# Feed-forward by seven products: the chain to one operand goes first, and twelve low parts go to GpSimd

## The chip, the cores and the metric

One core of a Trainium2 chip runs the whole program. The metric is the device time of one execution in microseconds (us); runs of one kernel are compared by their medians. The engines of the core work side by side, each through its own queue in order: TensorE (PE in the profile; its weight loads are PEld), VectorE (DVE), ScalarE (ACT), GpSimd (POOL) and SyncE (SP), which here only issues DMAs.

## The reference

One layer of a streaming encoder over 576 tokens (512 of a prompt and 64 of a sample): a combined projection, two kinds of attention, an output projection with a layer norm, a feed-forward block with a layer norm, and a gated embedding. All in float32. The part that the change touches is the feed-forward block:

```
x   = LN1(alpha * x + mix @ w_o)
hid = square(relu(x @ w_up))          # 1024 -> 4096
x   = LN2(alpha * x + hid @ w_down)   # 4096 -> 1024
```

## The kernel before

**Numbers.** TensorE multiplies float32 values as pairs: a high part (the value rounded by a copy to the matmul's type, made by ScalarE) and a low part (value minus high part, made by VectorE with one `tensor_tensor`). A product takes three matmuls per block of 128: weight high with operand high, weight high with operand low, weight low with operand high, in this order. Weights are split in the same way: a DMA brings a raw piece (`wraw`), ScalarE copies it to the high half of `whl` (line 149), VectorE makes the low half (line 155).

**Feed-forward groups.** The 4096 hidden values are worked in eight groups `g` of 512. Groups 0 and 1 go up by plain products. From then on the 2x2 block scheme with seven products in place of eight is used: an even and an odd group make a pair of row blocks, the token halves A and B (288 each) the columns. The stage runs over a list of "pairs" of output blocks, each with seven products of 12 matmuls: first four down-pairs of group 1, then for g = 2 and 4 two up-pairs of g, two up-pairs of g+1 and four down-pairs of g+1, then the four up-pairs of groups 6 and 7. Groups 6 and 7 go down by plain products.

The seven products of a pair come in the order `11, t0, t1, 21, t3, t2, 22`. On the operand's side they read these sums, each with a high and a low part:

```
ROWS = {"11": "11", "t3": "s1", "t0": "s3", "21": "12", "t1": "s2", "22": "s4", "t2": "22"}
```

For the down-pairs these sums are made of the hidden values by `operands` (line 1341): `11` and `s3` when the even group is done, and `s2`, `s1`, `22`, `12` and `s4` when the odd group's values come out, for each half `m` = 0, 1 of the group's columns (an up-pair each in groups 3 and 5). They lie in tiles `hA` (`s3`, `11`), `hB` (`12`, `22`), `hC` (`s1`, `s2`), `hD` (`s4`) and `hF` (the plain hidden values of the even group and running sums). The half m = 0 of an operand is read by the first six matmuls of a product, m = 1 by the last six.

The values of the second token half of an odd group come out of the product t2: line 1558 adds the last partial sum from PSUM (`r<-n,r`), line 1560 does relu and square in one VectorE instruction, line 1372 makes the sum s2 (`hF<-hF,r`), line 1351 copies its high part (ScalarE), line 1349 makes the low part (VectorE). Line 1374 makes s1, line 1379 makes s4 from `12` and the sum before, in place of `12`. In the down-pairs, lines 1585, 1587, 1596 and 1599 add products from PSUM to the layer's output `Y`.

**Order.** Two things set the order on each engine. The program emits these steps through a list (`later(delay, fn)`, up to three a clock, a clock being six matmuls), between them steps of the weights (`WT.step`), which also issue the loads: SP brings a raw piece, and GpSimd's queue issues a DMA that adds a second piece to it in place (line 210, one a pair). Then the framework's scheduler orders every engine's instructions at build time: of those that it reckons to be ready, the one written first goes first; inside `tc.high_priority()` they go ahead of the others. The matmuls of the seven products are pinned to the program's order. On the chip each engine takes its list in order and waits on semaphores.

Of the kernel before, what the change touches and what calls it, by code (L numbers as in the profile page):

```python
# [11 lines left out]
OP = mybir.AluOpType  # L12
# [24 lines left out]
def tile_hybrid_step(ctx: ExitStack, tc: tile.TileContext, I, O):  # L37
    nc = tc.nc
    PE, ACT, DVE, POOL, SP = nc.tensor, nc.scalar, nc.vector, nc.gpsimd, nc.sync
# [4 lines left out]
    def f(ap):  # L44
        return ap.bitcast(F32)
# [16 lines left out]
    def later(delay, fn):  # L62
        number[0] += 1
        evq.append((clock[0] + delay, number[0], fn))
# [52 lines left out]
    class Weights:  # L117
# [23 lines left out]
        def split(self, u, src, cuts, eng):  # L141
            lo_at = [0]

            def high(c):
                def fn():
                    if c is cuts[0]:
                        self.slot(u)
                        lo_at[0] = clock[0] + 2
                    ACT.copy(self.hv[u][:, 0, c], src["tile"][:, c])  # L149
                return fn  # L150

            def low(c):
                def fn():
                    t = self.hv[u]
                    eng.tensor_tensor(t[:, 1, c], src["tile"][:, c], f(t[:, 0, c]), OP.subtract)  # L155
                    if c is cuts[-1]:
                        self.done.add(u)
                return fn
            for c in cuts:
                self.piece(u, None, high(c), src)  # L160
            for c in cuts:
                self.piece(u, lo_at if len(cuts) == 1 else None, low(c), src)
# [1149 lines left out]
    HX, late = {}, []  # L1312

    def sets(g):

        if g >= G_DOWN:
            hid[g] = base.tile([128, 2, 4, NT], F32R, name="hidE", tag="AL") if g % 2 == 0 else \
                fb.tile([128, 2, 4, NT], F32R, name="hidO", tag="hidO")
            return
        names = ("s3", "11") if g % 2 == 0 else ("12", "22")  # L1320
        t = base.tile([128, 2, 2, 4, HW], F32R, name="hA", tag="AL") if g % 2 == 0 else \
            fb.tile([128, 2, 2, 4, HW], F32R, name="hB", tag="hidO")
        for i, n in enumerate(names):
            HX[n] = [t[:, i, x] for x in range(2)]
        if g % 2 == 0:
            HX["f"] = fs.tile([128, 2, 4, HW], F32, name="hF")
# [13 lines left out]
    def operands(g, m, t, v):  # L1340

        b = slice(2 * m, 2 * m + 2)
        tt = DVE.tensor_tensor

        def split(n, v, d=0):
            owed[n] = owed.get(n, 0) + 1

            def low():
                tt(HX[n][1][:, b], v, f(HX[n][0][:, b]), OP.subtract)
                owed[n] -= 1  # L1350
            later(d, lambda: ACT.copy(HX[n][0][:, b], v))
            later(d, low)

        if g >= G_DOWN:
            oh, ol = [hid[g][:, x, b, (A, B)[t]] for x in range(2)]
            later(0, lambda: ACT.copy(oh, v))
            later(0, lambda: DVE.tensor_tensor(ol, v, f(oh), OP.subtract))
            return
        F = [HX["f"][:, x, b] for x in range(2)]
        if g % 2 == 0:  # L1360
            if t == 0:
                split("11", v)
            if t == (g == 0):
                later(3, lambda: tt(F[0], F[0], F[1], OP.subtract))
                split("s3", F[0], 3)
            return
        if t == 1:
            if m == 0:
                later(0, more_sets)
                if g > 1:  # L1370
                    later(0, last_set)
            later(0, lambda: DVE.scalar_tensor_tensor(F[0], F[0], -1.0, v, op0=OP.mult, op1=OP.subtract))
            split("s2", F[0])
            later(1, lambda: tt(F[1], F[1], v, OP.subtract))
            split("s1", F[1], 1)
            split("22", v, 3)
            return
        split("12", v)
        later(2, lambda: tt(v, v, F[0], OP.add))
        if g > 1:  # L1380
            split("s4", v, 2)
        else:
            late.append(lambda: split("s4", v, 2))

    def up_half(g, c, m, sl):
        t = (A, B).index(sl)
        r = lnp[0].tile([128, 2, 320], F32, name="relu", bufs=2)[:, :, :HW]
        out = HX["f"][:, t, c:c + 2]
        later(0, lambda: ACT.activation(r, m[:, :, :HW], AF.Relu))
        later(0, lambda: ACT.activation(out, r, AF.Square))  # L1390
        operands(g, c // 2, t, out)

    def up_evac(g, c, m):
        if c == 0:
            HX["r"] = fs.tile([128, 2, 2, HW], F32, name="r", bufs=2)
        rr = HX["r"]
        r = rr[:, :, c]
        later(0, lambda: ACT.activation(r, m[:, :, :HW], AF.Relu))
        later(0, lambda: ACT.activation(r, r, AF.Square))
        if c:  # L1400
            for t in (1, 0):
                operands(g, 0, t, rr[:, t])

    def up(g, lns=None):
# [28 lines left out]
        for t in (1, 0):  # L1433
            m = psum_g()
            for c in range(2):
                for _ in gemm(m[:, c, :HW], Ws[c], range(8), BH, BL, (A, B)[t]):
                    WT.step()
                    yield 1
            later(0, lambda t=t, m=m: ACT.activation(rr[:, t], m[:, :, :HW], AF.Relu))
            later(0, lambda t=t: ACT.activation(rr[:, t], rr[:, t], AF.Square))  # L1440
            operands(g, 1, t, rr[:, t])
# [84 lines left out]
    def owe(P, fn):  # L1526
        def do():
            fn()
            P.left -= 1
        P.left += 1  # L1530
        later(0, do)

    def settle(P):
        while P.left:
            pop_now()

    def up_pair(g, m):

        P = Pair(U["P", g // 2, g % 2 * 2 + m], SX)
        b = slice(2 * m, 2 * m + 2)  # L1540
        tt = DVE.tensor_tensor
        if m == 0:
            P.start = lambda: sets(g)

        def target(t):
            return HX["f"][:, t, b] if g < G_DOWN and g % 2 == 0 else P.r[:, t]

        def t0():
            P.r = fs.tile([128, 2, 2, HW], F32, name="r", bufs=2)
            owe(P, lambda: ACT.copy(P.r[:, 1, 0], P.z))  # L1550

        def t3():
            settle(P)
            with tc.high_priority():
                tt(P.r[:, 1, 1], P.e, P.r[:, 1, 0], OP.subtract)

        def t2():
            tt(P.r[:, 1, 0], P.o, P.r[:, 1, 0], OP.add)
            if g % 2:
                later(0, lambda: DVE.scalar_tensor_tensor(target(1), P.r[:, 1], 0.0, P.r[:, 1], op0=OP.max, op1=OP.mult))  # L1560
            else:
                later(0, lambda: ACT.activation(P.r[:, 1], P.r[:, 1], AF.Relu))
                later(0, lambda: ACT.activation(target(1), P.r[:, 1], AF.Square))
            operands(g, m, 1, target(1))

        def s21():
            later(0, lambda: ACT.activation(P.r[:, 0, 0], P.d, AF.Relu))

        def s22():
            later(0, lambda: ACT.activation(P.r[:, 0, 1], P.e, AF.Relu))  # L1570
            later(0, lambda: ACT.activation(target(0), P.r[:, 0], AF.Square))
            operands(g, m, 0, target(0))
        P.posts = {"t0": t0, "21": s21, "t3": t3, "t2": t2, "22": s22}
        return P

# [257 lines left out]
```

## Time and profile before

| what | value |
|---|---|
| median of 3 runs | 765.87 us (765.47 to 766.1) |
| the profiled execution | 765.81 us, its span 764.1 us |
| TensorE busy | 751.4 us (98%) |
| VectorE busy | 571.4 us (75%) |
| ScalarE busy | 472.6 us (62%) |
| GpSimd busy | 110.6 us (14%) |

Busy time is the time in which an engine executes an instruction; waits on semaphores are not in it. The seven-product stage runs from 381.4 to about 653 us of the span. In the profile's rows a group is named by its line, engine, operation and tiles (`out<-in`); a row of the instructions in order of time begins with the start and the duration in us, and a bracket at its end gives the idle time before it and what ended it. Several like instructions in a row are merged (`x2`), and VectorE's instructions overlap by some 0.08 us where they follow each other at once, so the distance of their starts is a little less than their duration.

### The profile page before, as it was taken

Reading aid. Unit: us, or ns where it says so; the run is one execution under the profiler, and the core shown is the slowest. Engines: PE = TensorE matmul, PEld = TensorE weight load, DVE = VectorE, ACT = ScalarE, POOL = GpSimd, SP = SyncE. Lnnn points to the kernel's source line nnn. Section 1 sums busy time; section 2 is a strip of 40 time slices with the busy share of each in tenths; the row PEclk is TensorE's granted clock in tenths of the full one; section 3 lists DMA queues with packets and bytes.
Section 4 is the critical chain, followed back from the end, with each engine's and each line's share of the span. In section 5 each row is a group of like instructions: output and inputs, shape, how many; then the busy total and the mean of one; then the engine's idle time right before and its main releaser. Section 6 shows DMA issues by size and latency. Waiting matters only on the chain.

```text
span 764.1 us, 14624 instructions
## 1 busy us (share of the span) xinstructions
PE 751.4 (98%) x5679; PEld 730.8 (96%) x5679; DVE 571.4 (75%) x1119; ACT 472.6 (62%) x931; POOL 110.6 (14%) x130
## 2 busy tenths in 40 slices
PE   9999999999999999999999999999999999999997
PEld 7999988999899999999999999999999999999997
DVE  6788888888777866779777579866898766657643
ACT  6589777897676535797654577435764466525451
POOL 7100324344241000100000000000000000011000
PEclk9999999999999999999999999999999999999999
DMA  8538354245222325352447666667667664731001
GB/s 284 171 69 152 125 141 121 91 138 173 88 86 81 110 64 174 116 171 86 111 111 178 148 158 175 147 161 184 157 143 181 152 151 152 286 113 30 28 29 69
DMA packets 38197, 101.35 MB, mean 133 GB/s; under 512 B 6000, under 2 KB 10224, under 8 KB 38000
## 3 DMA queue, kind: packets, MB, share of 16 engines
q1 hardware_dynamic: 34384, 87.61, 37.5%
q0 software_dynamic: 3456, 12.58, 10.2%
q8 instruction: 44, 0.72, 0.4%
q10 hardware_dynamic: 288, 0.22, 0.1%
q14 instruction: 25, 0.20, 0.1%
HBM read 85.26 MB, written 9.54 MB: 124 GB/s over the span
## 4 chain that ended last, share of the span: by engine, by line
PE 77%; DVE 13%; ACT 8%; issue 2%; DVEq 0%; ACTq 0%
PE g L288 40%; PE m L288 14%; PE n L288 13%; PE T L56 2%; DVE dbias L693 2%; ACT xr L771 2%; DVE whl L155 2%; DVE m L691 1%; PE V L958 1%; ACT whl L149 1%; PE m L452 1%; DVE sP L891 1%; PE m L466 1%; DVE x L774 1%; PE S L883 1%
## 5 line engine op out<-in xcount | busy, mean ns | idle before, releaser
L149 ACT CAST whl<-wraw 128x1024 fp32r<-128x1024 f32 (+2 forms) x190 | 154.9, 828 | 80.9 <-PE g L288 46.3
L155 DVE TENSOR_TENSOR whl<-wraw,whl 128x1024 fp32r<-128x1024 f32 (+2 forms) x158 | 157.7, 1008 | 53.3 <-ACT whl L149 52.6
L288 PE MATMUL m<-AH,whl 128*128 128x288 f32 x736 | 176.7, 307 | 0.0
L288 PE MATMUL g<-BH,whl 128*128 128x288 f32 (+2 forms) x768 | 160.0, 298 | 0.0
L288 PEld LDWEIGHTS m<-AH,whl 128*128 128x128 f32 x736 | 126.4, 188 | 1.7 <-issue 1.0
L288 PEld LDWEIGHTS g<-BH,whl 128*128 128x128 f32 x768 | 125.0, 188 | 1.5 <-ACT BH L1229 0.2
L288 PE MATMUL g<-BL,whl 128*128 128x288 f32 (+2 forms) x384 | 113.6, 296 | 0.6 <-DVE BL L1233 0.6
L288 PE MATMUL m<-AL,whl 128*128 128x288 f32 x368 | 108.8, 296 | 0.0
L288 PEld LDWEIGHTS g<-BL,whl 128*128 128x128 f32 x384 | 72.3, 188 | 1.2 <-DVE BL L1233 1.1
L288 PEld LDWEIGHTS m<-AL,whl 128*128 128x128 f32 x368 | 69.5, 189 | 0.7
L210 POOL DMA_DIRECT2D wraw<-in_w_dram x24 | 20.7, 864 | 287.5 <-DMA wraw<-in_w_dram 184.8
L896 ACT ACTIVATE sP<-sP,st 128x128 f32<-128x128 f32 (+4 forms) x72 | 39.4, 549 | 35.1 <-DVE st L891 35.0
L155 POOL TENSOR_TENSOR whl<-wraw,whl 128x512 fp32r<-128x512 f32 x32 | 42.2, 1333 | 89.2 <-ACT whl L149 85.0
L288 PE MATMUL m<-BH,whl 128*128 128x288 f32 x192 | 42.9, 302 | 0.0
L288 PE MATMUL g<-s,whl 128*128 128x288 f32 x288 | 42.1, 295 | 0.0
L288 PE MATMUL n<-BH,whl 128*128 128x288 f32 x192 | 42.0, 294 | 0.0
L288 PEld LDWEIGHTS g<-s,whl 128*128 128x128 f32 x288 | 39.5, 188 | 0.0
L56 PE MATMUL T<-ident,sP 128*128 128x128 f32 (+1 forms) x176 | 31.3, 274 | 1.5 <-DVE sP L905 0.6
L288 PEld LDWEIGHTS m<-BH,whl 128*128 128x128 f32 x192 | 32.0, 188 | 0.5 <-issue 0.3
L288 PEld LDWEIGHTS n<-BH,whl 128*128 128x128 f32 x192 | 32.0, 188 | 0.0
L1505 ACT ACTIVATE g<-n 128x288 f32<-128x288 f32 x24 | 9.5, 395 | 35.6 <-PE n L288 35.6
L288 PE MATMUL m<-BL,whl 128*128 128x288 f32 x96 | 28.3, 295 | 0.0
(327 smaller groups left out, 1624.1 us busy)
## 6 DMA issues: line engine op xcount, KB each, us to landing
wraw<-in_w_dram SPq DMA_DIRECT2D x48, 512.0 KB, 3.8
wraw<-in_w_dram POOLq DMA_DIRECT2D x24, 512.0 KB, 5.8
wraw<-in_w_qkv_dram SPq DMA_DIRECT2D x23, 512.0 KB, 3.6
wraw<-in_w_dram SPq DMA_DIRECT2D x24, 256.0 KB, 4.3
wraw<-in_w_up_dram SPq DMA_DIRECT2D x8, 512.0 KB, 4.1
wraw<-in_w_down_dram SPq DMA_DIRECT2D x8, 512.0 KB, 4.2
wraw<-in_w_gate_dram SPq DMA_DIRECT2D x8, 512.0 KB, 4.5
wraw<-in_w_o_dram SPq DMA_DIRECT2D x8, 384.0 KB, 3.0
```

Source lines behind the costliest of these rows:

```text
L56: PE.transpose(out, in_, ident[:n, :n])
L149: ACT.copy(self.hv[u][:, 0, c], src["tile"][:, c])
L155: eng.tensor_tensor(t[:, 1, c], src["tile"][:, c], f(t[:, 0, c]), OP.subtract)
L210: POOL.dma_start(t[:, :n], it["acc"], accum_op=OP.add)
L288: mm = PE.matmul(ps, W(w, kw, wc), a[:, ka, cols], start=(first and i == 0), stop=(last and i == n - 1), skip_group_check=more)
L452: PE.matmul(mk[:, h, :HW], w0(part, k), a[:, k, h * HW:(h + 1) * HW], start=(k == 0 and i == 0), stop=(k == 7 and i == 2))
L466: PE.matmul(acc[b][:n[b], :304], a[:, k, b * 128:b * 128 + n[b]], ixw(part, k), start=(k == 0 and i == 0), stop=(k == 7 and i == 2))
L691: tc.keep_in_program_order(DVE.max(m, s))
L693: tc.keep_in_program_order(DVE.match_replace(out=s, in_to_replace=m, in_values=s, imm_value=GONE))
L771: q(lambda r=r, s=s: ACT.mul(v2(xr[r * 32:r * 32 + 32]), v[s * 32:s * 32 + 32], sc))
L896: ACT.activation(j["P"], j["P"], AF.Exp, bias=j["st"][:, 0:1], scale=-1.0, accum_out=j["st"][:, 2:3])
L1505: ACT.mul(P.e, P.o, -1.0)
```

## The change

In `operands`, a helper `split` gets two switches: the engine that makes the low part, and `soon`, which puts the two instructions of the split under high priority. Of the odd groups (1, 3 and 5), the sum s2 (line 1372 before) and its two parts are put under high priority. The low parts of `12` and `s4` are made by GpSimd in place of VectorE. In `up_pair`, for odd groups, the addition at line 1558 and the relu-square at line 1560 are put under high priority too. What is computed, the matmuls, the tiles and the order in which the program emits all this stay as they were.

```diff
-        def split(n, v, d=0):
+        def split(n, v, d=0, eng=DVE, soon=False):
             owed[n] = owed.get(n, 0) + 1
+            put = tc.high_priority if soon else ExitStack
+
+            def high():
+                with put():
+                    ACT.copy(HX[n][0][:, b], v)
 
             def low():
-                tt(HX[n][1][:, b], v, f(HX[n][0][:, b]), OP.subtract)
+                with put():
+                    eng.tensor_tensor(HX[n][1][:, b], v, f(HX[n][0][:, b]), OP.subtract)
                 owed[n] -= 1
-            later(d, lambda: ACT.copy(HX[n][0][:, b], v))
+            later(d, high)
             later(d, low)
...
-            later(0, lambda: DVE.scalar_tensor_tensor(F[0], F[0], -1.0, v, op0=OP.mult, op1=OP.subtract))
-            split("s2", F[0])
+            def s2():
+                with tc.high_priority():
+                    DVE.scalar_tensor_tensor(F[0], F[0], -1.0, v, op0=OP.mult, op1=OP.subtract)
+            later(0, s2)
+            split("s2", F[0], soon=True)
             later(1, lambda: tt(F[1], F[1], v, OP.subtract))
             split("s1", F[1], 1)
             split("22", v, 3)
             return
-        split("12", v)
+        split("12", v, eng=POOL)
         later(2, lambda: tt(v, v, F[0], OP.add))
         if g > 1:
-            split("s4", v, 2)
+            split("s4", v, 2, POOL)
         else:
-            late.append(lambda: split("s4", v, 2))
+            late.append(lambda: split("s4", v, 2, POOL))
...
         def t2():
-            tt(P.r[:, 1, 0], P.o, P.r[:, 1, 0], OP.add)
+            with tc.high_priority() if g % 2 else ExitStack():
+                tt(P.r[:, 1, 0], P.o, P.r[:, 1, 0], OP.add)
             if g % 2:
-                later(0, lambda: DVE.scalar_tensor_tensor(target(1), P.r[:, 1], 0.0, P.r[:, 1], op0=OP.max, op1=OP.mult))
+                def sq():
+                    with tc.high_priority():
+                        DVE.scalar_tensor_tensor(target(1), P.r[:, 1], 0.0, P.r[:, 1], op0=OP.max, op1=OP.mult)
+                later(0, sq)
```

## The prediction

> **What bounds the kernel now.** I read the head of the page first, then the chain that ended last in order of time, then TensorE's waits in the seven-product stage, then the table of stretches around the places that the chain shows, and last the instructions there one by one.
>
> ```profile
> span 764.1 us, 14624 instructions
> PE 751.4 (98%) x5679; PEld 730.8 (96%) x5679; DVE 571.4 (75%) x1119; ACT 472.6 (62%) x931; POOL 110.6 (14%) x130
> ```
>
> TensorE is the bound, and the change neither adds nor removes a matmul. So all that it can win is time in which TensorE stands still. In the chain, the stage that the change touches is a run of matmuls with two breaks:
>
> ```profile
> 473.46 1.17 ACT hB L1351 x2
> 475.24 1.43 DVE hC L1349 x2
> ...
> 484.44 2.88 DVE whl L155 x3
> ...
> 566.73 1.43 DVE hC L1349 x2
> ...
> 575.92 2.88 DVE whl L155 x3
> ```
>
> The two breaks are 91.5 us apart and are the same event: group 3, and then group 5, ends its up-products and its down-products begin. TensorE's waits from 330 to 655 us name the same two causes, the operand hC and a weight low part whl, twice each:
>
> ```profile
> PE n L288 <- DVE whl L155: 1.1, 2, 0.5
> PE n L288 <- DVE hC L1349: 0.8, 2, 0.4
> ```
>
> These waits are idle time with modelled ends, so I size the stalls by starts instead. From the instructions in order of time, TensorE at the first break:
>
> ```profile
> 471.04 1.75 PE L288 MATMUL n<-hA,whl 128*128 128x288 f32 x12
> 472.63 1.75 PE L288 MATMUL g<-hA,whl 128*128 128x288 f32 x12
> 474.21 1.45 PE L288 MATMUL n<-hC,whl 128*128 128x288 f32 x7
> 476.05 0.93 PE L288 MATMUL n<-hC,whl 128*128 128x288 f32 x5 [0.39 <-DVE hC L1349]
> 476.82 1.76 PE L288 MATMUL g<-hB,whl 128*128 128x288 f32 x12
> ...
> 486.39 0.43 PE L288 MATMUL n<-hC,whl 128*128 128x288 f32 x2
> ...
> 488.80 1.50 PE L288 MATMUL g<-hB,whl 128*128 128x288 f32 x10
> ```
>
> A product of 12 matmuls takes 472.63 - 471.04 = 1.59 us when nothing is late, 0.133 us a matmul. Product t1 took 476.82 - 474.21 = 2.61 us, so stall 1 is about 1.0 us: seven matmuls ran and the eighth, the first that reads the low part of s2 for m=1, waited. The t1 of the next pair took 488.80 - 486.39 = 2.41 us, so stall 2 is about 0.8 us: two matmuls ran and the third, the first that reads the low part of its weights, waited. That makes 1.8 us a break and 3.6 us in all, 0.5% of the run. This is the most that the change can win. (The profiled execution took 765.81 us, 1.7 us more than its span; the median of the runs shown is 765.87 us, so both sums can be made against 765.8.)
>
> Who is late is seen in the table of stretches (columns: PE, PEld, DVE, ACT, POOL):
>
> ```profile
> 460.00:471.00 11.00, 11.00 (x85) 11.00 (x84) 10.93 (x17) 8.66 (x15) 0.86 (x1) 1.00 0.58 146
> 471.00:483.00 12.00, 11.52 (x85) 11.07 (x84) 11.89 (x18) 7.19 (x12) 0.84 (x1) 1.00 0.61 154
> 494.00:505.00 11.00, 11.00 (x85) 11.00 (x84) 7.77 (x13) 4.39 (x6) 0.85 (x1) 1.00 0.67 167
> ```
>
> VectorE is 75% busy over the span but full here (10.93 of 11, 11.89 of 12), and back at 7.77 of 11 two pairs later. Stall 2 comes from this backlog: the chain runs on VectorE from 475.24 to 487.3 almost without a gap. GpSimd does nothing there but issue one DMA a pair.
>
> **The change part by part.** *The s2 chain goes first.* The path to stall 1 on VectorE before:
>
> ```profile
> 470.28 0.45 DVE L1558 TENSOR_TENSOR r<-n,r 128x288 f32<-128x288 f32 x1
> 470.65 1.21 DVE L155 TENSOR_TENSOR whl<-wraw,whl 128x1024 fp32r<-128x1024 f32 x1
> 471.78 0.75 DVE L1560 SCALAR_TENSOR_TENSOR r<-r 128x576 f32<-128x576 f32 x1
> 472.45 0.68 DVE L155 TENSOR_TENSOR whl<-wraw,whl 128x512 fp32r<-128x512 f32 x1
> 473.06 0.75 DVE L1372 SCALAR_TENSOR_TENSOR hF<-hF,r 128x576 f32<-128x576 f32 x1
> 473.72 0.75 DVE L1374 TENSOR_TENSOR hF<-hF,r 128x576 f32<-128x576 f32 x1
> 474.39 0.75 DVE L1349 TENSOR_TENSOR hB<-r,hB 128x576 fp32r<-128x576 f32 x1
> 475.24 1.43 DVE L1349 TENSOR_TENSOR hC<-hF,hC 128x576 fp32r<-128x576 f32 x2
> ```
>
> The chain is L1558, L1560, L1372, the ScalarE copy, the first L1349 on hC. Between its links stand two weight low parts (1.13 and 0.60 us by the distance of starts) and, while ScalarE copied hB first, L1374 and an hB low part. Put first, the chain passes the weight parts: 470.65 + 2 x 0.67 = 472.0 for L1372's end, 0.6 for the copy, 0.7 for the low part, about 473.4 to 474 against 474.21 + 7 x 0.133 = 475.1 when it is read. Stall 1 would go with about 1 us to spare. What is passed comes later by up to 2 us; the 1024-wide weight part, for the same t1, is read at 474.5 and ends at about 473.2 to 473.5. By itself, though, this only changes the order in a full queue. The work ahead of the weight part of stall 2 is not less, TensorE reaches it 1.0 us sooner, and it then waits 1.8 us there. I cost the ordering alone at nothing, to be paid at stall 2.
>
> *Twelve low parts go to GpSimd:* six of "12" (half of the hB row) and six of s4 (the hD row).
>
> ```profile
> L1349 DVE TENSOR_TENSOR hB<-r,hB x12: 747/750/754, 372.3 to 568.1; 128x576 fp32r<-128x576 f32 x12
> L1349 DVE TENSOR_TENSOR hD<-r,hD x6: 748/749/759, 380.9 to 570.2; 128x576 fp32r<-128x576 f32 x6
> L1154 POOL TENSOR_TENSOR ln_s<-ln_s,Y 128x576 f32<-128x576 f32 x1 | 1.4, 1444 | 0.6 <-ACT Y L1281 0.6
> ```
>
> VectorE gives up 12 x 0.75 = 9.0 us (0.67 each back to back) and GpSimd takes 12 x 1.44 = 17.3 us. Four of them fall into each break: 2.7 us off VectorE. If GpSimd ran beside VectorE for nothing, the backlog would end 2.7 us sooner, more than the 1.8 us, and both stalls would be gone.
>
> But the two do not run beside each other. Where both read two operands from SBUF, this trace shows one of them standing until the other ends:
>
> ```profile
> 147.27 2.59 POOL L155 TENSOR_TENSOR whl<-wraw,whl 128x512 fp32r<-128x512 f32 x2 [6.45 <-ACT whl L149]
> 148.63 1.84 DVE L773 TENSOR_TENSOR xr<-xr,sinT 128x576 f32<-128x576 f32 x1
> L773 DVE TENSOR_TENSOR xr<-xr,sinT x8: 748/749/1841, 148.6 to 245.5; 128x576 f32<-128x576 f32 x8
> ...
> 669.38 1.23 DVE L155 TENSOR_TENSOR whl<-wraw,whl 128x1024 fp32r<-128x1024 f32 x1
> 669.44 2.31 POOL L1152 TENSOR_TENSOR ln_s<-Y 128x512 f32<-128x512 f32 x1 [46.13 <-ACT whl L149]
> ```
>
> L773 takes 0.75 us, but 1.84 when it starts under a GpSimd instruction: GpSimd ended at 149.86, L773 0.61 later. The other way round, the GpSimd add of 669.44 ran until 671.75, 1.15 after VectorE's 1.23 us were over. So a moved low part costs VectorE between -0.67 us (its 1.44 lie wholly under work that does not clash) and 1.44 - 0.67 = +0.77 us (VectorE stands all the while). For the four of a break: -2.7 to +3.1 us. VectorE's instructions with one PSUM input do not clash:
>
> ```profile
> 311.54 1.45 POOL L1152 TENSOR_TENSOR ln_s<-Y 128x576 f32<-128x576 f32 x1 [71.45 <-ACT Y L1281]
> 312.06 2.75 DVE L1184 TENSOR_TENSOR Y<-Y,n 128x576 f32<-128x576 f32 x4 [2.57 <-PE n L1180]
> ```
>
> The four L1184 took 0.69 each under it. In a break such work (L1555, L1558, L1585, L1596, L1599: eight of them from 464 to 487 us, 0.37 each as L1558 by the distance of starts) is about 3 us of 23, mostly near the last of the four. I take +0.7, +0.3, +0.7 and -0.2, +1.5 us in all, nearer the upper end because the queue is full of two-operand instructions.
>
> The Trainium skill, "SBUF — State Buffer", section "Who interferes with whom", states this as an exclusive lock: a VectorE instruction with two SBUF inputs and a GpSimd instruction that reads SBUF block each other for the whole instruction; the trace agrees (1.84 against 0.75 us above). By that rule alone, with no cover, the four would cost +3.1 us a break; without it they would win 2.7.
>
> *The two together, walked through one break.* The "12" part of m=0 holds VectorE from about 464.6 to 466.0, the s4 part from 468.7 to 470.1. The weight part that began at 469.15 then ends near 471.3 (read at 472.9, no stall). L1558 and the chain come about 1.8 us later than without the clash, the low part of s2 ends near 475.4 against 475.1: 0.3 us left of stall 1. On ScalarE the copy of "12" for m=1 now stands behind the hoisted copy and ends near 476.7 (it was one of the two at 473.39), so GpSimd ends its low part at about 478.2; product 21 reads it at 475.8 + 0.3 + 8 x 0.133 = 477.0: a new stall of up to 1.2 us. With TensorE that late, and the s4 part of m=1 partly under L1585 and L1596, the weight part of the next t1 is just in time. Sum about 1.5 to 1.6 us a break against 1.8: -0.4 us in all.
>
> *GpSimd's queue.* Its only other work here is the accumulating DMA, one a pair:
>
> ```profile
> wraw<-in_w_dram POOLq DMA_DIRECT2D x24, 512.0 KB, 5.8
> ...
> 474.56 0.84 POOL L210 DMA_DIRECT2D wraw<-in_w_dram  x1 [11.66 <-DVE hF L1374]
> ```
>
> The program writes an issue two pairs ahead: the one of 474.56 is for the pair that starts near 494, and it lands after 5.8 us, at 480.4. Some 10 us are to spare, so a low part ahead of an issue delays no product: nothing charged. SP's plain loads wait for the same buffers to be read by VectorE's weight parts; what these slip, 1 to 2 us, lies under the same 10 us. A low part behind one waits: the issue of 474.56 waits until its first load has landed, and a "12" part behind it starts at 475.4 at the earliest and ends at 476.9, on the edge of its need. If that cover is gone it is the stall of up to 1.2 us that I have already charged. Group 1 has the same four parts near 375 to 389 us, where TensorE did not wait; I charge nothing, with up to 0.5 us if its "12" part for m=1 slips.
>
> **The rivals.** *Both stalls go (33%).* Against it stands the clash; for it, that the queue's order is made new at build time with twelve instructions fewer for VectorE, and that in the order before, two other weight parts stood ahead of the late one (the three L155 at 484.44), so 1.1 us can be won by order alone. It gives 765.8 - 3.6 = 762.2 at the limit, 763 if half a microsecond a break stays.
>
> *The clash decides: slower (27%).* One mechanism: in the full queue from 456 to 487 us VectorE stands through most of the four GpSimd instructions. Stall 1 may go, but the weight parts end later by the loss. It decides from where the loss exceeds 0 (below that the change wins), and is measurable from 0.8 us a break. At the upper end, 3.1 us a break, 765.8 + 6.2 = 772.0; at +1.5, without the relief that the walk found, 768.8. The rule of the skill named above speaks for it.
>
> *The ordering does nothing, the stall only changes its name (40%, my forecast).* Stall 1 goes over to the "12" part or to stall 2: within 0.2%, 764.3 to 767.3, by the walk 765.4.
>
> **How the numbers follow.** 0.2% is 1.5 us, about what a measurement of this kernel can tell from no change (three runs spread over 0.6 us). The likeliest case gives 765.4. Its own range is 764.3 to 767.3. Eight in ten: from 762.6 (nearly all of the 3.6 us) to 768.8 (the clash at +1.5 a break uncovered). Faster 0.33, within 0.40, slower 0.27.
>
> **What would show it.** Right: L1349 on GpSimd x12 near 1.45 us, with a maximum near 2 us where it waited; VectorE's L155 and L1349 with maxima near 2 us near 465 to 485; the wait for hC gone or under 0.3 us; a wait of TensorE for hB on GpSimd, or a longer one for whl. Wrong towards faster: no row of TensorE waiting there, and GpSimd's parts under L1585 and L1596. Wrong towards slower: t1 of the second pair over 3.4 us from its start to the next product's.

## The result and the profile after

| kernel | median | runs |
|---|---|---|
| before | 765.88 us | 4 runs |
| after | 773.32 us | 772.15, 772.2, 774.44, 775.19 |

The ratio is 1.0095 [1.0083, 1.0108]: the change costs 7.4 us, 1%. The forecast was 765.4 us with a range to 768.8; the time lies above it. The runs that took longer had the lower granted clock: 0.998 in the two of 772.2 us, 0.992 in that of 774.44, 0.990 in that of 775.19. The profiled execution took 772.2 us, span 770.5. The head of its page:

```profile
span 770.5 us, 14642 instructions
PE 752.8 (98%) x5679; PEld 732.4 (95%) x5679; DVE 572.8 (74%) x1107; ACT 473.2 (61%) x931; POOL 133.1 (17%) x142
```

VectorE has twelve instructions fewer and is busy 1.4 us longer than before. Twelve times 0.75 us went away, so some 10 us were added to the others. GpSimd took on 22.5 us for twelve instructions, 1.88 each, not 1.44. (In the kernel after, the low part is line 1355; lines 1558, 1372 and 1374 of before are 1568, 1380 and 1383.) TensorE's waits from 330 to 670 us:

```profile
PE n L288 <- DVE hC L1355: 5.2, 2, 2.6
PE n L288 <- ACT hC L1351: 0.6, 2, 0.3
```

The wait for whl is gone, the one for hC is over six times as long as before. TensorE at the two breaks, by instructions in order of time (start, duration, in brackets the idle time before):

```profile
475.11 0.96 PE L288 MATMUL n<-hC,whl 128*128 128x288 f32 x6
476.37 0.40 PE L288 MATMUL n<-hC,whl 128*128 128x288 f32 x1 [0.29 <-ACT hC L1351]
479.34 0.93 PE L288 MATMUL n<-hC,whl 128*128 128x288 f32 x5 [2.57 <-DVE hC L1355]
480.11 2.91 PE L288 MATMUL g<-hB,whl 128*128 128x288 f32 x12
482.81 2.18 PE L288 MATMUL g<-hC,whl 128*128 128x288 f32 x12
484.83 1.76 PE L288 MATMUL n<-hB,whl 128*128 128x288 f32 x12
...
569.70 0.96 PE L288 MATMUL n<-hC,whl 128*128 128x288 f32 x6
570.95 0.40 PE L288 MATMUL n<-hC,whl 128*128 128x288 f32 x1 [0.29 <-ACT hC L1351]
573.93 0.94 PE L288 MATMUL n<-hC,whl 128*128 128x288 f32 x5 [2.58 <-DVE hC L1355]
574.70 1.76 PE L288 MATMUL g<-hB,whl 128*128 128x288 f32 x12
...
580.21 1.06 PE L288 MATMUL g<-hD,whl 128*128 128x288 f32 x6 [0.55 <-DVE Y L1609]
```

In both breaks t1 takes 5.00 us (480.11 - 475.11, 574.70 - 569.70) where an undisturbed product takes 1.59: stall 1 is 3.4 us, up from 1.0. In the first break the next two products also run slowly without a wait, 2.70 and 2.02 us: together 1.5 us too long. In the second they take 1.60, but product 22 waits 0.7 us for an addition to Y. Stall 2 is gone. Group 1, which had no stall before, now has one of about 0.8 us. It comes by lateness: VectorE's sum in place of `12` (line 1388) waits until GpSimd has read `12`, ScalarE's copy of `s4` waits for the sum, and the ScalarE instruction of line 1514, for which TensorE waits, stands behind that copy in ScalarE's queue:

```profile
386.72 0.76 DVE L1388 TENSOR_TENSOR r<-r,hF 128x576 f32<-128x576 f32 x1 [0.96 <-POOL hB L1355]
387.51 0.67 ACT L1351 CAST hD<-r 128x576 fp32r<-128x576 f32 x1 [2.75 <-DVE r L1388]
388.54 1.86 PE L288 MATMUL g<-hC,whl 128*128 128x288 f32 x12 [0.52 <-ACT g L1514]
```

The losses are 3.4 + 1.5, 3.4 + 0.7 and about 0.8 us in group 1, 9.8 in all. Before it was 3.6. The difference of 6.2 us covers that of the spans, 6.4.

**Who made the low part of s2 late.** The low parts of after, by tile (count, shortest/median/longest in ns):

```profile
L1355 DVE TENSOR_TENSOR hC<-hF,hC x12: 744/746/1959, 375.0 to 573.8; 128x576 fp32r<-128x576 f32 x12
L1355 POOL TENSOR_TENSOR hB<-r,hB x6: 1692/1850/1919, 371.9 to 571.6; 128x576 fp32r<-128x576 f32 x6
L1355 DVE TENSOR_TENSOR hB<-r,hB x6: 745/747/1994, 376.3 to 574.5; 128x576 fp32r<-128x576 f32 x6
L1355 POOL TENSOR_TENSOR hD<-r,hD x6: 1417/1662/4458, 379.1 to 576.7; 128x576 fp32r<-128x576 f32 x6
```

GpSimd and then VectorE in the first break, in order of time:

```profile
465.12 1.92 POOL L1355 TENSOR_TENSOR hB<-r,hB 128x576 fp32r<-128x576 f32 x1 [1.30 <-PE g L288]
469.11 1.85 POOL L1355 TENSOR_TENSOR hD<-r,hD 128x576 fp32r<-128x576 f32 x1 [2.07 <-ACT hD L1351]
476.15 0.86 POOL L210 DMA_DIRECT2D wraw<-in_w_dram  x1 [5.19 <-DVE hF L1380]
476.97 1.69 POOL L1355 TENSOR_TENSOR hB<-r,hB 128x576 fp32r<-128x576 f32 x1
```
```profile
465.66 1.99 DVE L1355 TENSOR_TENSOR hB<-r,hB 128x576 fp32r<-128x576 f32 x1
...
470.31 2.86 DVE L155 TENSOR_TENSOR whl<-wraw,whl 128x1024 fp32r<-128x1024 f32 x2 [0.29 <-ACT whl L149]
473.10 0.45 DVE L1568 TENSOR_TENSOR r<-n,r 128x288 f32<-128x288 f32 x1
...
474.85 0.76 DVE L1380 SCALAR_TENSOR_TENSOR hF<-hF,r 128x576 f32<-128x576 f32 x1
...
476.19 1.22 DVE L155 TENSOR_TENSOR whl<-wraw,whl 128x1024 fp32r<-128x1024 f32 x1
477.32 2.62 DVE L1355 TENSOR_TENSOR hC<-hF,hC 128x576 fp32r<-128x576 f32 x2
```

Each of the three GpSimd instructions lies on a lengthened VectorE instruction, which ends about as long after it as that instruction takes by itself, back to back: GpSimd ended at 467.04, 470.96 and 478.66; the hB part at 467.65, the first of the two L155 near 472.0, the first hC part at 479.28. They cost 1.24 us (1.99 against 0.75), about 0.5 (2.86 for two that take 1.22 + 1.13 = 2.35 back to back) and 1.2 us (2.62 against 1.43). So the chain starts at 473.10, 2.0 us ahead of t1 (before: 3.9), and is held again at its last link. And the chain was not first: a 1024-wide weight part (476.19) stands between line 1380 and the low part of s2. From L1568 to that low part's end it takes 6.2 us (473.10 to 479.28), where the old order took 5.7 (470.28 to 475.99); without the block of 1.2 us it would be 5.0.

### The profile page after: what moved, and what is told of

Same layout as the page of the kernel before. It is cut to its first block, busy times and chain, and to the rows that moved or that the text cites. A ratio compares the mean times of both kernels' runs of the same rounds, so it can differ in the third digit from the quotient of the medians.

```text
span 770.5 us, 14642 instructions
## 1 busy us (share of the span) xinstructions
PE 752.8 (98%) x5679; PEld 732.4 (95%) x5679; DVE 572.8 (74%) x1107; ACT 473.2 (61%) x931; POOL 133.1 (17%) x142
## 4 chain that ended last, share of the span: by engine, by line
PE 75%; DVE 15%; ACT 7%; issue 2%; POOL 0%; DVEq 0%; ACTq 0%
PE g L288 38%; PE m L288 14%; PE n L288 12%; DVE whl L155 2%; PE T L56 2%; PE V L958 2%; DVE dbias L693 2%; ACT whl L149 2%; ACT xr L771 1%; DVE m L691 1%; DVE hC L1355 1%; PE m L452 1%; DVE sP L891 1%; PE m L466 1%; PE S L883 1%
## 5 line engine op out<-in xcount | busy, mean ns | idle before, releaser
L155 DVE TENSOR_TENSOR whl<-wraw,whl 128x1024 fp32r<-128x1024 f32 (+2 forms) x158 | 159.2, 1016 | 56.9 <-ACT whl L149 56.1
L155 POOL TENSOR_TENSOR whl<-wraw,whl 128x512 fp32r<-128x512 f32 x32 | 42.3, 1335 | 90.1 <-ACT whl L149 74.9
L1152 POOL TENSOR_TENSOR ln_s<-Y 128x576 f32<-128x576 f32 (+2 forms) x3 | 5.1, 1699 | 137.9 <-ACT Y L1281 71.5
```

## The experiments

The theory: two-operand work on both engines holds VectorE (the lock), in an order that the priorities do not improve, and a long idle stretch then lowers TensorE's clock. The main rivals: the priorities themselves do harm; GpSimd is merely too slow at its twelve parts; the lowered clock has another cause.

**Priorities alone.** All low parts back on VectorE, `high_priority` kept.

```diff
-        split("12", v, eng=POOL)
+        split("12", v)
...
-            split("s4", v, 2, POOL)
+            split("s4", v, 2)
...
```

> The high-priority half of the change alone; all low parts on VectorE. Theory (the time went to GpSimd's twelve low parts, and the priorities move nothing): 765.9 us, within 0.1% of before, with the same waits of TensorE for hC and whl, 1.0 and 0.8 us a break. Rival (the new order itself costs, or the order alone would have won): 3 us or more away from before, or stall 1 gone and stall 2 near 1.8 us.

Measured: 765.79 us (8 runs), 1.000 [0.999, 1.001]. The order that the build makes of it is that of the kernel before on all five queues, instruction by instruction. So by itself this half of the change does nothing at all. No run moves the twelve parts without the priorities; but the kernel after, built without its four new priorities, gives the same program as with them (a build, not a run). So the whole loss belongs to the twelve moved parts.

**GpSimd writes only.** As after, but each moved low part is replaced by three memsets on GpSimd: the subtraction is left out and those low parts are zero.

```diff
-                    eng.tensor_tensor(HX[n][1][:, b], v, f(HX[n][0][:, b]), OP.subtract)
+                    if eng is POOL:
+                        for _ in range(3):
+                            POOL.memset(f(HX[n][1][:, b]), 0.0)
+                    else:
+                        tt(HX[n][1][:, b], v, f(HX[n][0][:, b]), OP.subtract)
```

> The changed kernel, but GpSimd's twelve low parts are left out: in each one's place stand three memsets of the same part, which take about as long and read nothing from SBUF. VectorE's, ScalarE's and TensorE's queues stay as in the changed kernel. Theory (GpSimd's reads block VectorE's two-operand instructions): no VectorE instruction is stretched (maximum of L1355 on hC and hB under 0.8 us), the stall at t1 falls from 3.4 to under 1 us, and the time is 762.5 to 764.5 us. Rival (the order of VectorE's queue, the same as in the changed kernel, brings the stall): 770 us or more, with the same wait for hC. Rival (GpSimd is late with its parts, not in VectorE's way): the wait for hC stays, waits for hB or hD go.

Measured: 763.7 us (7 runs), 0.9972 [0.9961, 0.9982]. VectorE's order is that of after but for one addition to Y, and no low part of hB or hC on it takes longer than 0.75 us. TensorE's only wait of the stage:

```profile
PE n L288 <- DVE hC L1359: 1.0, 2, 0.5
```

In the first break:

```profile
474.15 1.10 PE L288 MATMUL n<-hC,whl 128*128 128x288 f32 x7
...
476.51 1.76 PE L288 MATMUL g<-hB,whl 128*128 128x288 f32 x12
```

Product t1 takes 2.36 us: with nothing blocked, the order of after still leaves 0.8 us of stall 1. The chain (line 1568 of after) starts at 470.69 here, 3.5 us ahead of t1.

The memsets ran earlier than the low parts would have (they wait for less, none ran from 460 to 490 us), so this shows what the moved work is worth when GpSimd keeps out of the way: 2.1 us gained. It does not show a writing GpSimd beside VectorE. The other 9.6 us up to after come with GpSimd's subtractions: the block, their later start, and what follows from both; this run doesn't divide them.

**GpSimd repeats, VectorE keeps its work.** Before, plus the twelve subtractions done once more by GpSimd into a scratch tile.

```diff
                 tt(HX[n][1][:, b], v, f(HX[n][0][:, b]), OP.subtract)
+                if twice:                # set for "12" and s4
+                    POOL.tensor_tensor(scratch(), v, f(HX[n][0][:, b]), OP.subtract)
...
```

> The kernel before, with VectorE's queue unchanged, and GpSimd does the twelve subtractions a second time into a scratch tile that nobody reads. Theory (block): VectorE loses up to 1.45 us for each of the four GpSimd instructions of a break and gains nothing, so 4 to 6 us a break at two breaks, 771 to 778 us, with VectorE instructions of near 2 us. Rival (GpSimd costs only because the path waits for its results, or through the queue's order): 766 us as before, since nobody waits for the scratch tile but the sum in place of 12.

Measured: 778.67 us (4 runs), 1.0171 [1.0155, 1.0186]. VectorE, ScalarE and TensorE have before's order, and the results that GpSimd makes are read by nobody. Yet 12.8 us are lost (the granted clock was 0.993 over the span, so some of it is the clock, below). By the starts of the same matmuls each of the two breaks loses about 4.5 us, as expected, and group 1, which the expectation left out, 4.6. One of the twelve, and the VectorE instruction that overwrites its input:

```profile
481.36 3.41 POOL L1354 TENSOR_TENSOR sc<-r,hB 128x576 bf16<-128x576 f32 x1
...
484.81 0.76 DVE L1384 TENSOR_TENSOR r<-r,hF 128x576 f32<-128x576 f32 x1 [1.30 <-POOL sc L1354]
```

GpSimd was held for some 2 us under a row of VectorE instructions, and then VectorE waited 1.30 us for GpSimd to have read. So the lock costs in both directions, by blocking and by lateness, and the sum in `r` (s4 made in place of `12`) passes the lateness back to VectorE's queue.

**Only s4 on GpSimd, only "12" on GpSimd.** After with the calls of `split` for one of the two without the engine.

```diff
# s4 alone
-        split("12", v, eng=POOL)
+        split("12", v)
# "12" alone
-            split("s4", v, 2, POOL)
+            split("s4", v, 2)
...
```

> The changed kernel with only s4's low parts on GpSimd; 12's are VectorE's again. Theory (block): two GpSimd instructions a break in place of four, the last of them beside instructions that read PSUM: between the two, 766 to 769 us, with stall 1 near 1.5 us and no stretched low part of s2. Rival (12 alone does the harm through its late result): 765 to 766 us.

Measured: 765.21 us (10 runs), 0.9992 [0.9983, 1.0001]; TensorE's waits:

```profile
PE n L288 <- DVE hC L1355: 2.5, 2, 1.2
```

Stall 1 grows from 1.0 to 1.5 us (by starts), stall 2 is gone: by the trace 0.3 us a break less, 0.6 in all. The interval of the ratio just includes 1.

> Only the six low parts of "12" are made by GpSimd; s4's six stay on VectorE. Theory (the two engines block each other when both read SBUF pairs, and the "12" beside the low part of s2 m=1 is the harmful one): the long VectorE low part of hC stays (about 2.0 us), the wait of TensorE for hC stays at 2 times 1.2 to 2.6 us, and most of the loss is here: 768 to 773 us, against 765.2 with s4's parts alone. Rival 1 (it takes all twelve: the chain's late start comes from s4 m=0 beside the weight parts): without them the chain starts as early as before and the time is 764.5 to 766. Rival 2 (the loss is the clock that drops after a long idle stretch, whatever caused it): the break without a drop shows the same stall as the changed kernel's group 5, and the time depends on the phase: 768 or 772.

Measured: 768.89 us (5 runs), 1.0033 [1.0020, 1.0047]. In its first break:

```profile
476.59 3.80 POOL L1355 TENSOR_TENSOR hB<-r,hB 128x576 fp32r<-128x576 f32 x1
```
```profile
477.83 0.94 PE L288 MATMUL n<-hC,whl 128*128 128x288 f32 x5 [1.06 <-DVE hC L1355]
...
480.44 0.94 PE L288 MATMUL g<-hB,whl 128*128 128x288 f32 x5 [0.75 <-POOL hB L1355]
```

"12" is the harmful half, +2.6 us, but not by what I expected: the low part of s2 is not lengthened; here GpSimd is the one that is held (3.80 us beside a row of VectorE instructions), and the stall at product 21 that the prediction had named shows, 0.75 us. Another 0.5 us a break is lost ahead of t1, and stall 2 is gone here too. The two halves do not add up: -0.6 and +2.6 us against +7.4 together. In after both the chain's late start (a part of s4 at 469.11) and the blocked low part (a "12" part at 476.97) fall on the same stall, and it becomes long enough for what follows. The whole of the difference is not worked out.

**The lowered clock.** Before, with two or three instructions added to the s2 chain of m = 1 in groups 3 and 5; each is max(F, F), which changes no value. GpSimd does nothing new, but the build reorders a few neighbours on VectorE and ScalarE.

```diff
+            if m and g > 1:
+                for _ in range(2):          # or 3
+                    later(0, lambda: DVE.scalar_tensor_tensor(F[0], F[0], 1.0, F[0], op0=OP.mult, op1=OP.max))
             split("s2", F[0])
```

> The kernel before with two instructions added to the chain of s2 in the second up-pair of groups 3 and 5: the maximum of F with itself, which leaves F as it is. In the built queue the low part of s2 stands four VectorE instructions later, 2.7 us, without any work on GpSimd: a stall of TensorE of about 3.1 us by the bracket, where the changed kernel had 2.6. If the lowered clock behind the break belongs to the idle stretch itself, it shows here too, by chance of position: clock 0.5 to 0.8 for some us behind one break or both, times spread over 2 us or more, 769.7 to 774. If it belongs to GpSimd's work or to something else in the changed kernel, the clock stays at 1.00 in both breaks and all times lie within 1 us of each other at 769.5 to 771.5.

> The same with three such instructions: the low part of s2 stands six VectorE instructions later, 4.0 us, and the stall is about 4.4 us by the bracket. If the idle stretch lowers the clock: it does so in both breaks or more often than with two, some 1.5 us of extra time for each, 772 to 777 us. If not: 772 to 774, all runs within 1 us, clock 1.00.

Measured: 772.29 us (771.02, 771.18, 773.41, 774.1) with two, 1.0079 [1.0063, 1.0095]; 775.35 us (774.56 to 775.99) with three, 1.0116 [1.0101, 1.0132]. TensorE at stall 1 of the first break, with two and then with three:

```profile
477.13 0.42 PE L288 MATMUL n<-hC,whl 128*128 128x288 f32 x1 [2.06 <-ACT hC L1351]
478.44 1.57 PE L288 MATMUL n<-hC,whl 128*128 128x288 f32 x5 [0.89 <-DVE hC L1349]
```
```profile
479.10 0.40 PE L288 MATMUL n<-hC,whl 128*128 128x288 f32 x1 [3.40 <-ACT hC L1351]
480.40 1.13 PE L288 MATMUL n<-hC,whl 128*128 128x288 f32 x5 [0.91 <-DVE hC L1349]
```

The clock falls in both breaks of both kernels, without any new work on GpSimd. So it belongs to the idle stretch. Where exactly it changes is read from stretches of 0.2 us (columns: TensorE busy, its granted clock, DMA share, GB/s); of after, of two added, of three added:

```profile
480.20:480.40 0.20, 0.20 (x3) 0.78 0.92 184
483.60:483.80 0.20, 0.20 (x3) 0.69 0.00 0
```
```profile
477.20:477.40 0.20, 0.20 (x1) 0.96 1.61 225
484.20:484.40 0.20, 0.20 (x3) 0.97 0.00 0
572.80:573.00 0.20, 0.15 (x1) 0.89 0.42 82
```
```profile
480.80:481.00 0.20, 0.20 (x3) 0.86 0.10 20
```

Between a fall and the return every stretch has 0.50. A mean of 0.78 means 0.44 of the 0.2 us at half clock, so after falls at 480.31 and is back at 483.72: 3.41 us. With two added it falls at 477.38 and is back at 484.21: 6.83 us, twice 3.41; again 572.96 to 579.78, 6.83. With three: 480.94 to 484.36, 3.42. The two falls of the kernel with two added lie 95.57 us apart, 28 times 3.413. So the clock is set on a fixed grid of 3.41 us, for a whole step at a time. What decides is how much of one step TensorE stood idle. By starts and durations, in the step ahead of the fall: 2.4 us in after (476.90 to 479.34), 2.06 with two added (475.07 to 477.13), 2.5 with three. In steps without a fall: 1.83 with three added (475.70 to 477.53, the step ahead of that), and in the second break of after 1.41 and 1.45 us, since there the grid's border, 27 steps on from the fall at 572.47, cuts the same stall in two. The run with GpSimd's repeats narrows it: its clock falls at 394.16, 482.91 and 578.48 (26 and 28 steps apart), and in the step ahead of the second of these TensorE stood idle for 0.98 + 0.90 = 1.88 us, in two pieces:

```profile
480.92 0.40 PE L288 MATMUL n<-hC,whl 128*128 128x288 f32 x1 [0.98 <-ACT hC L1356]
482.22 1.02 PE L288 MATMUL n<-hC,whl 128*128 128x288 f32 x5 [0.90 <-DVE hC L1352]
```

So in these runs the limit lies between 1.83 and 1.88 us of 3.41, as far as the modelled ends of the matmuls can tell.

The Trainium skill, "TensorE: Matmul & The Clock Gate", Part 1, describes this: a free-running window of 3413 ns, half clock after an idle window, full clock after a busy one. The window agrees to the last digit shown. "Idle" is less strict here than the page's one idle window: 1.88 us, 55% of it, were enough.

**Order by edges.** Before, with all low parts on VectorE, and `tc.issue_after` in place of priorities: an edge puts an instruction behind another of the same engine in the built order, whatever the scheduler reckons.

```diff
+        if kind == 3 and x and ("s2", 1) in ref:           # low half of the 512-wide weight part
+            return tc.issue_after(ref["s2", 1])
...
+        if kind == 0 and ("W2", x) in ref:                 # W2: third weight part of the unit before
+            st.enter_context(tc.issue_after(ref["W2", x]))
+        if kind == 0 and x and ("s2", 1) in ref:           # low half of a unit's first weight part
+            st.enter_context(tc.issue_after(ref["s2", 1]))
...
+        if n in ("12", "22") and ("s2", x) in ref:         # high part x = 0, low part x = 1
+            return tc.issue_after(ref["s2", x])
...
-                tt(y, y, ps, op)
+                with tc.issue_after(ref["s2", 1]), tc.issue_after(ref["W2", 1]):
+                    tt(y, y, ps, op)
```

A unit is the weights of one pair: four parts, made of three raw pieces and two sums of them.

> The kernel before with every low part still on VectorE, and the order set by explicit edges instead of priorities: the 512-wide weight part, the next unit's first weight part, the additions to Y and the parts of "12" and "22" stand behind the parts of s2; in the down-pairs the third weight part of a pair goes before the first of the next. In the built queue S2 now follows sq at once, with one weight part between it and the low part of s2 m=1, where three instructions stood before. Theory (order is what the two stalls hang on, and there is enough of VectorE's time): stall 1 falls from 1.0 to 0.0 to 0.3 us and stall 2 from 0.8 to 0 to 0.3 in both breaks, so 762.3 to 763.5 us. Rival 1 (VectorE is full there, so what is put behind comes late at the next product): the wait reappears as one for hB or for whl, 765 to 766. Rival 2 (the low part of the weights now stands behind t2 and its high part, late by itself): t1 of the first pair waits for whl, 764.5 to 767.

Measured: 767.1 us (11 runs), 1.0011 [1.0002, 1.0020]. The time is not shorter. Stall 1 falls to 0.5 us by starts, but the edges of m = 0 delayed weights and cost 0.4 us ahead of the break, and at stall 2:

```profile
487.30 0.53 PE L305 MATMUL n<-hC,whl 128*128 128x288 f32 x2 [0.48 <-ACT g L1530]
488.27 1.60 PE L305 MATMUL n<-hC,whl 128*128 128x288 f32 x10 [0.43 <-DVE whl L170]
```

Rival 2 of its expectation: the third weight part's copy waits for the second sum of weights (line 184 before), which stood behind a weight part with time to spare.

> The same edges, and s4's low parts on GpSimd (six, as in the run with s4 alone). Theory (s4's parts run beside PSUM-reading or unhurried work, so they cost VectorE little and take 1.4 us a break off it): both stalls at 0 to 0.3 us, 762.0 to 763.2, 0 to 0.5 us under the run with edges alone. Rival (the lock): a GpSimd part of s4 beside t1, t2 or the weight parts stretches one of them to about 2 us in each break and a stall of 0.5 to 1.2 us comes back: 763.5 to 766.

Measured: 767.24 us (11 runs), 1.0013 [1.0004, 1.0021]. The old stalls are 0.6 and 0.3 us by starts, and a new one appears, the low part of "12" in VectorE's own queue:

```profile
PE g L305 <- DVE hB L1375: 1.4, 2, 0.7
```

Next, edges for m = 1 alone, and the two sums of weights ahead of the unit's second weight part. In these two kernels the low part of a unit's first weight part is taken from its tile after the sum t1 has been added to it, so their results are false and they stand here for their times alone. Number and size of the instructions are unchanged.

```diff
-            self.split(u + 1, r1, [all2], DVE)
             self.piece(u + 1, None, t1, r1, r2)
             self.piece(u + 2, None, t2, r2)
+            self.split(u + 1, r1, [all2], DVE)
```

> Edges again, all low parts on VectorE, but for the second pair alone (m=1), and the two sums of weights of a unit now stand ahead of its second weight part. The run with edges everywhere had lost 0.8 us before its first break and its stall 2 had grown, since the third weight part's high part waited for the second sum of weights. Theory: the built queue now has S2, S1, low part of s2, low part of "12" in a row and the third weight part ahead of the 512-wide one; stall 1 at 0 to 0.3, stall 2 at 0 to 0.4 us in both breaks and nothing lost before: 763.0 to 764.5 us (with before at 765.9). Rival (VectorE is full, the wait only moves on): a wait of 0.3 to 0.8 us for hB or for whl appears in each break and the time is 765 to 766.5.

> The same with s4's six low parts on GpSimd. Theory: 1.4 us a break less on VectorE, so at most the time of the run with edges alone, 762.5 to 764.5 us. Rival (lock): a low part of s4 beside a weight part stretches it to about 2 us and 0.5 to 1.2 us a break come back: 764.5 to 766.5.

Measured: 763.59 us (5 runs), 0.9963 [0.9950, 0.9975]; with s4 on GpSimd 765.38 (11 runs), 0.9989 [0.9980, 0.9997]. The edges win 2.6 us; moving s4's parts on top gives 1.8 back. There product 22 waits 1.0 us in both breaks for an addition to Y on VectorE; in the first, GpSimd's part (1.82 us) lies on the two weight parts ahead of that addition, which take 3.06 us together. The last kernel has the same edges without s4 on GpSimd and takes the sums in a place where no low part reads its tile after them:

```diff
-            self.split(u + 1, r1, [all2], DVE)
-            self.piece(u + 1, None, t1, r1, r2)
-            self.piece(u + 2, None, t2, r2)
+            self.split(u + 1, r1, [all2], DVE, between=((u + 1, (r1, r2), t1), (u + 2, (r2,), t2)))
```

Here `between` puts both sums between the high and the low part of u + 1, behind the low part of u.

> The kernel before with explicit edges for m=1 and all low parts on VectorE, as in e9_pins_m1, but with the two sums of weights placed between the first weight part's low part and the second's, so that no sum comes ahead of a low part that reads the same tile (in e9_pins_m1 the first weight's low part read its tile after the sum; the work is the same in kind and number). The built queue of TensorE is that of e9_pins_m1, and VectorE's differs in the order of a few neighbours. Theory (the order is what the stalls hang on): the time of e9_pins_m1, 763.0 to 764.2 us beside before at 765.9 to 766.3, a ratio of 0.995 to 0.998; stall 1 gone in both breaks, a wait for whl of 0.2 to 0.4 us at most in place of stall 2. Rival (its gain came from the sums of weights being ahead of the loads they now wait for, by chance of neighbours): 765 to 766.5 us.

Measured: **762.25 us** (762.18 to 762.8, 5 runs), 0.9955 [0.9941, 0.9969], the fastest of all. The rows of TensorE's waits from 330 to 670 us are gone to the last one, and the products of the first break follow at 1.60 us, but for one of 1.78 (483.40 to 485.18):

```profile
473.81 1.77 PE L303 MATMUL n<-hC,whl 128*128 128x288 f32 x12
475.41 1.76 PE L303 MATMUL g<-hB,whl 128*128 128x288 f32 x12
...
483.40 1.94 PE L303 MATMUL g<-hA,whl 128*128 128x288 f32 x12
485.18 1.77 PE L303 MATMUL n<-hC,whl 128*128 128x288 f32 x12
```

VectorE is busy 571.3 us here, 571.4 before: no work went anywhere. By the starts of the same matmuls each break is 1.6 us shorter, 3.2 in both; the two profiles differ by another 0.4 us within their first 100 us, ahead of this stage. The low part of s2 now starts at 473.69, the third instruction behind relu-square where it was the fifth. No run moves the sums without the edges, so what each of the two is worth alone stays open.

## Why the prediction was wrong, step by step

- **TensorE is the bound and 3.6 us are all there is to win: right.** The last kernel gains 3.9 us by the medians (2.4 to 4.5 by the interval), 3.2 of them seen in the two breaks, and has no wait left.
- **The s2 chain goes first: wrong in its premise.** The chain was not moved past the weight parts; the priorities alone left every queue as it was. So the price of nothing for them came out right by luck. That order alone has to be paid at stall 2 was wrong too: the last kernel wins both stalls with order alone, from a queue that I had called full. It was full of work in the wrong sequence.
- **The walk to stall 1 ("0.3 us left"): the step that failed.** Its start was right: the chain's first link came 1.9 us late beyond the 0.9 us that TensorE itself was behind by then (473.10 against 470.28); 1.8 had been forecast. But from there to the end of the low part of s2 the walk had about 3.3 us, and it took 6.2. Of the 2.9 us more, 1.6 are the two weight parts that were not passed (0.6 for the one between lines 1568 and 1572, and 1.0 for the end of the other, from 476.31, when ScalarE's copy was done, to 477.32). The other 1.2 us are the block by the "12" part of m = 1, which lay on the low part of s2 itself; the walk had charged that part at product 21 alone, with its own lateness. The run with memsets shows the share of the order: 0.8 us of stall 1 without any block. The rest up to 3.4 us is the blocks, 1.2 us on the last link and a chain that starts 2.0 us ahead of t1 in place of 3.5.
- **Twelve low parts to GpSimd, +1.5 us a break: too much as VectorE's time, and not what it depends on.** The lock was there, as expected. The four parts of the first break held VectorE for 1.24, 0.5, 1.2 and 0 us, 2.9 together, and took 2.7 us of work off it: about +0.3 net, where +0.7, +0.3, +0.7 and -0.2 stood in the sum. What counted was where a block fell: on the last link of the chain it delayed TensorE as well. I also took 1.44 us for a part on GpSimd; it took 1.4 to 4.5, since it was held as well.
- **The sum of a break, 0.3 us at stall 1 and up to 1.2 at product 21: wrong for after.** It has 3.4 at stall 1 and none at 21, which came too late to wait; then 1.5 us of half clock in the first break, and 0.7 at product 22 in the second: 4.9 and 4.1. For the kernel with "12" alone the stall at 21 was right (0.75 us).
- **Stall 2: right that it goes** when the four parts leave VectorE; it also goes when either half does.
- **GpSimd's queue: right.** No product waited for a load, and the DMA issue of 476.15 held the "12" part for under 0.1 us: ScalarE's copy of `12` (476.22) ended at 476.89, the part began at 476.97. **Group 1:** up to 0.5 us forecast, about 0.8 measured, by the sum in place of `12`.
- **The rivals.** "The clash decides" named the direction, but put the loss into the weight parts, one us of VectorE for one of time. Its price without relief was 768.8, its limit 772.0. All four runs lie above the limit, by 0.2 to 3.2 us. A term that the prediction didn't have at all is the clock: 1.5 us for the step at half clock in the profiled run, which no row of before could show, since no stall there is longer than 1.0 us. Without it that run would be at 770.7. The two longer runs, with clocks of 0.992 and 0.990, probably hold more of it; their traces were not kept.
- **What would show it.** "Wrong towards slower" was to be read at t1 of the second pair; it showed at t1 of the first. The VectorE maxima near 2 us came as written, but as signs of the loss; GpSimd's parts took 1.85 and 1.66 us in the median and 4.46 at most, not 1.45 and 2.

Why the priorities changed nothing is argued, not shown: the scheduler orders those instructions that it reckons ready, and the weight parts seem to be ready before the chain's next link is. That edges move the same instructions fits this.

## What to carry to other kernels

Before moving work from a full engine to an idle one, ask what the two share: here a low part taken off VectorE at 0.75 us came back as up to 1.2 us of blocking, and its result came late as well. Look first for order: in the same full queue, edges that let only the instructions with time to spare stand behind the urgent chain, together with an earlier place for two sums of weights, were worth 3.9 us, while priorities were worth nothing here. And keep TensorE's idle time within any 3.4 us well under the 1.88 us that lowered the clock here; it cost another 1.5 us or more.

## What the hardware showed that was not expected

- TensorE's granted clock changed only on a fixed grid of 3.41 us and stood at 0.50 for one or two whole steps (3.41 and 6.83 us). 1.88 us of idle time within one step were enough, 1.83 were not; the same stall of after cost 1.5 us more in one break and nothing more in the other, by where the grid's border lay. The clock stayed low for a second step where TensorE had stood idle for 0.89 or 0.76 us of the first, and came back after one step in the six cases without idle time in it.
- GpSimd, once behind VectorE, can be held through several back-to-back two-operand instructions: 3.41, 3.80 and 4.46 us for a part that took 1.42 at its shortest.
